# A hybrid decoder layer on one core: two tiles of the in-projection become a fifth Strassen pair, and quadrants of pairs are used from their banks

## The chip, the cores and the metric

The kernel runs on one core of a Trainium2 chip. The core has a matrix engine (TensorE, here PE, with its weight loads PEld), a vector engine (VectorE, DVE), a scalar engine (ScalarE, ACT), a general engine (GpSimd, POOL) and a queue that issues most DMAs (SyncE, SP). Each engine works off its own list of instructions in order; between engines there are semaphores. The metric is the device time of one execution in microseconds (us).

## What is computed

One layer over 1024 tokens of width 1024, in float32. The parts that matter here, shortened from the reference:

```python
u = rms_norm(x, norm1_g)
z = u @ w_in                       # 1024 -> 3584 columns, 28 tiles of 128
cb, cc, ch = split(z[:, :1536], 3) # convolution group, 512 each
rq, rk, rv, rg = split(z[:, 1536:], 4)
y_conv = cb * causal_dwconv3(cc * ch, conv_w)   # three taps along the tokens
y_conv = group_rms_norm(y_conv, conv_norm_g, 8)
o = chunkwise_retention(rotary(rq), rotary(rk) / sqrt(128), rv)   # 4 heads
y_ret = group_rms_norm(o, ret_norm_g, 4) * silu(rg)
x = x + concat(y_conv, y_ret) @ w_out
x = x + relu(rms_norm(x, norm2_g) @ w_up)**2 @ w_down
out = rms_norm(x, final_norm_g)
```

## The kernel before

Everything is held transposed: a tile is 128 columns of a product (on the partitions) by 1024 tokens, worked on in two halves of 512 tokens. A float32 product is made of three matmuls on high and low parts (hi x hi, hi x lo, lo x hi). A group of 12 matmuls is four k-tiles of 128 times these three, over 512 tokens; it is the unit of the order (the constant SLOT), and a weight piece of 128 x 512 (tile r, split into wh by ACT and wl by DVE or POOL) feeds one or more groups. A whole tile of the in-projection takes four groups: two halves by two of k. Two tiles can be made together with a 2 x 2 Strassen scheme (`pair_in`): seven products of one group each in place of eight groups, at the price of sums and differences of the weight pieces (POOL and DVE) and of the quadrants (DVE). A quadrant is one tile's half; n1 to n7 below are the seven products, taken in the order 1, 2, 5, 6, 3, 7, 4, alternately in banks of the pools pm and pr, of four banks each.

The input is not normalised before the projection; each token's norm factor is multiplied in behind it. R holds the factor of each token, R2 its square (in the buffer named ssq). So the gate takes z*R before its silu, b takes z*R, and the product c*h takes R2 once. The tiles 0 to 11 of the convolution come as c, h, b for each of four output tiles (f % 3 = 0, 1, 2); 12 to 19 are q and k; 20 to 23 are the gates of the four heads. IN_TURNS lists the turns behind q and k: 0, 1, 2, 3 and 20 as whole tiles, then four pairs, then tile 21; IN_END lists tiles 22 and 23, of which all first halves are made before the second halves. Beside the first turns PE works on the retention of heads 2 and 3; its small steps (transposes of line 663, tiny DVE operations on tile m for the heads' norm) stand between the groups.

What follows a tile runs in tasks: `conv_h` makes c*h*R2 and the three taps (cv), `conv_b` makes b*R*cv and asks for a group norm, `gate` makes the silu and multiplies it into the head's output o_n, `norm` makes a group's norm with two matmuls on PE (lines 483, 484) and a correction by DVE. `background` and `tick` set the order in which the tasks' steps are written behind each group, by a model clock of each engine; `yield (pool, dve)` leaves the engine to that model. The lists of the engines are then fixed.

The buffers for whole tiles are short, so o_n of heads 2 and 3 and the first two convolution outputs y0 and y1 are written to DRAM (`put_by`, tile sp) and fetched again (`get_back`, tile back). Before, all four returns stand behind pair (10, 11), ahead of tile 21. The out projection starts with the high and low parts yh and yl of all eight y, made by `split_y`; its first group takes y0 to y3, y0 first. Nearly every operation of ACT, DVE and POOL goes through the class Engine, whose line 74 the profile shows for it; nearly every matmul through `mm`, line 403; weight pieces are fetched at line 162.

Of the kernel before, what the change touches and what calls it, by code (L numbers as in the profile page):

```python
# [16 lines left out]
P = 128  # L17
# [22 lines left out]
IN_TURNS = [0, 1, 2, 3, 20, (4, 5), (6, 7), (8, 9), (10, 11), 21]  # L40
IN_END = [22, 23]
# [38 lines left out]
def hybrid_layer(  # L80
# [594 lines left out]
    a_of, cvs = {}, {}  # L675

    def conv_h(i, half, z, psum):

        a, sl = a_of[i], hs[half]
        eng = dve if psum else (yield (pool, dve))  # L680
        eng.tensor_mul(a[:, sl], a[:, sl], z)
        eng = yield (pool, dve)
        eng.tensor_mul(a[:, sl], a[:, sl], R2[:, sl])
        mark(("a", i, half), eng)
        if half:
            yield "a", i, 0
        yield (act,)
        if i not in cvs:
            cvs[i] = unit(s="cv")
        cv = cvs[i]  # L690
        w = [sm[:, CW + 3 * i + j : CW + 3 * i + j + 1] for j in range(3)]
        act.activation(cv[:, sl], a[:, sl], AF.Copy, scale=w[2])
        yield (dve,)
        for j in (1, 2):
            to = slice(max(sl.start, j), sl.stop)
            dve.scalar_tensor_tensor(
                cv[:, to], a[:, to.start - j : to.stop - j], w[2 - j], cv[:, to],
                ALU.mult, ALU.add,
            )
        mark(("cv", i, half), dve)  # L700

    def conv_b(i, half, z, out, psum):
        sl = hs[half]
        o = out[:, sl]
        eng = dve if psum else (yield (pool, dve))
        eng.tensor_mul(o, z, R[:, sl])
        yield "cv", i, half
        eng = yield (pool, dve)
        eng.tensor_mul(o, o, cvs[i][:, sl])
        y[i] = out  # L710

        def done(rt, less):
            yield (dve,)
            dve.scalar_tensor_tensor(o, o, less_g[:, i : i + 1], rt, ALU.mult, ALU.mult)
            yield (dve,)
            dve.scalar_tensor_tensor(o, less, 1.5, o, ALU.subtract, ALU.mult)
            mark(("y", i, half), dve)

        asked.append((o, blkr, 1.0 / 64, done, clock[eng], LATE * half))

    def gate(h, half, z, g, psum):
        sl = hs[half]
        eng = dve if psum else (yield (pool, dve))
        eng.tensor_mul(g[:, sl], z, R[:, sl])
        yield (act,)
        act.activation(g[:, sl], g[:, sl], AF.Silu)
        yield "o", h, half
        yield (dve,)
        o = o_n[h, half]
        dve.scalar_tensor_tensor(  # L730
            o[:, sl], g[:, sl], sm[:, RG + h : RG + h + 1], o[:, sl], ALU.mult, ALU.mult
        )
        y[4 + h] = o
        mark(("y", 4 + h, half), dve)

    def use(f, half, out, z, psum):

        if f >= 20:
            return gate(f - 20, half, z, out, psum)
        if f % 3 == 1:  # L740
            return conv_h(f // 3, half, z, psum)
        return conv_b(f // 3, half, z, out, psum)

    def whole(f):
        def evac(z):
            if f < 20 and f % 3 == 0:
                out = a_of[f // 3] = unit(s="a")
                for half, sl in enumerate(hs):
                    act.copy(out[:, sl], z[half])
                return  # L750
            out = None if f < 20 and f % 3 == 1 else unit(s="z")
            for half in range(2):
                spawn(use(f, half, out, z[half], True), clock[dve])

        tile_in(evac)
# [68 lines left out]
    def pair_in(fs):  # L824
        out = [unit(s="z") for _ in range(2)]
        (c11, c12), (acc, c22) = ([o[:, sl] for sl in hs] for o in out)
        for at, n in enumerate(UP_ORDER):
# [6 lines left out]
            ready = None  # L834
            if n == 1:
                act.copy(acc, b)
            if n == 2:
                dve.tensor_add(c11, acc, b)
                ready = 0, 0
            if n == 5:  # L840
                b5 = b
            if n in (6, 7, 4):
# [3 lines left out]
            if n == 7:  # L846
                dve.tensor_add(c22, acc, b5)
                ready = 1, 1
            if n == 3:
                dve.tensor_add(c12, c12, b)  # L850
                ready = 0, 1
            if n == 4:
                ready = 1, 0
            if ready:
                f, half, o = fs[ready[0]], ready[1], out[ready[0]]
                if f < 20 and f % 3 == 0:
                    a_of[f // 3] = o
                else:
                    spawn(use(f, half, o, o[:, hs[half]], False), clock[dve], LATE * half)
# [35 lines left out]
    for at, turn in enumerate(IN_TURNS):  # L895
        if isinstance(turn, tuple):
# [3 lines left out]
        if at == len(IN_TURNS) - 2:  # L900
            for h in (2, 3):
                force(("by", ("o", h)))
                o_n[h, 0] = o_n[h, 1] = get_back(("o", h))
            for i in range(2):
                force(("by", ("y", i)))
                y[i] = get_back(("y", i))
                got["back", i] = now[0] + 10.0
# [3 lines left out]
    for half in range(2):  # L911
        for f, (z, banks, pieces) in ends.items():
            for c in range(2):
# [10 lines left out]
                if c:  # L924
                    spawn(use(f, half, z, banks[half], True), clock[dve])
# [638 lines left out]
```

## Time and profile before

| | |
|---|---|
| three runs | 1071.92, 1071.01, 1069.68 us; median 1071.01 |
| profiled execution | 1070.03 us, span of its instructions 1068.1 us |
| granted clock of PE | 0.999 |
| busy in the span | PE 1054.8, PEld 879.2, DVE 870.8, ACT 463.6, POOL 561.6 us |
| pair (8, 9), pair (10, 11), tile 21, out projection begin at | 272.4, 291.4, 311.43, 344.97 us |

A row of a timeline gives start and length in us, engine, line, operation, what it writes <- what it reads, the shape, xN where N instructions of the kind follow each other, and in brackets how long the engine stood idle before and for whom. A row by groups gives count | busy us, mean ns of one | idle us before them. In rows on a tile the figures are ns, least/median/most. A row on DMAs gives the us from issue to landing, least/median/most.

### The profile page before, as it was taken

To read this page: it belongs to the slowest core of one execution; us is meant where nothing else is said; L and a number is where in the kernel's file an instruction comes from. 1 tells how busy PE (TensorE), PEld (TensorE's weight loads), DVE (VectorE), ACT (ScalarE), POOL (GpSimd) and SP (SyncE) were. 2 spreads that over 40 slices of the span, in tenths; PEclk is the share of its full clock that TensorE was granted. 3 is DMA by queue.
4 is the path that set the end of the run, shared out by engine and by line. 5 is a ranking of instruction groups with operands and counts; after the bars stand their busy time and mean duration, and the time that the engine had idled before them with its cause. 6 is when DMAs were issued, how large, how long until landed. Compare 5 with 4: busy or idle time off the path is not lost.

```text
span 1068.1 us, 13853 instructions
## 1 busy us (share of the span) xinstructions
PE 1054.8 (99%) x4860; PEld 879.2 (82%) x4860; DVE 870.8 (82%) x1231; ACT 463.6 (43%) x906; POOL 561.6 (53%) x381
## 2 busy tenths in 40 slices
PE   9999999999999999999999999999999999999997
PEld 8888888788888888788788888888888888888886
DVE  7446546799998665799999989999899899899955
ACT  8211445673437444443343433343443434334453
POOL 6334324367854233559458267277186295384552
PEclk9999999999999999999999999999999999999999
DMA  7121122122223733051221211211301201200204
GB/s 276 65 58 42 38 80 70 63 95 80 69 69 129 256 115 123 11 187 39 61 59 49 79 31 50 90 30 50 99 21 50 89 21 49 90 21 19 69 30 158
DMA packets 39685, 82.25 MB, mean 77 GB/s; under 512 B 4544, under 2 KB 5696, under 8 KB 39616
## 3 DMA queue, kind: packets, MB, share of 16 engines
q1 hardware_dynamic: 39328, 80.85, 23.5%
q8 instruction: 38, 0.62, 0.2%
q10 hardware_dynamic: 288, 0.52, 0.1%
q14 instruction: 31, 0.25, 0.1%
HBM read 71.92 MB, written 9.44 MB: 76 GB/s over the span
## 4 chain that ended last, share of the span: by engine, by line
PE 90%; DVE 6%; ACT 2%; issue 1%; POOL 1%; DVEq 0%; ACTq 0%; POOLq 0%
PE b L403 55%; PE b L1277 23%; PE b L357 4%; PE b L1386 4%; DVE t L74 1%; DVE wl L74 1%; DVE x L74 1%; DVE m L74 1%; ACT h L74 1%; DVE q L74 1%; DVE V L74 1%; PE b L339 0%; PE b L595 0%; PE b L1436 0%; PE b L246 0%
## 5 line engine op out<-in xcount | busy, mean ns | idle before, releaser
L74 ACT CAST wh<-r 128x512 fp32r<-128x512 f32 x286 | 176.6, 620 | 326.4 <-PE b L403 134.4
L403 PE MATMUL b<-U,wh 128*128 128x512 f32 x1024 | 315.8, 390 | 2.0 <-DVE x L74 1.2
L74 DVE TENSOR_TENSOR wl<-r,wh 128x512 fp32r<-128x512 f32 x250 | 232.8, 933 | 89.0 <-ACT wh L74 87.8
L74 POOL TENSOR_TENSOR r<-r,r 128x512 f32<-128x512 f32 x136 | 210.2, 1548 | 114.1 <-DVE wl L74 66.1
L1277 PE MATMUL b<-V,wh 128*128 128x512 f32 x784 | 242.0, 389 | 0.7 <-POOL V L74 0.4
L403 PEld LDWEIGHTS b<-U,wh 128*128 128x128 f32 x1024 | 191.7, 188 | 43.2 <-issue 2.4
L74 DVE TENSOR_TENSOR x<-x,b 128x512 f32<-128x512 f32 (+1 forms) x312 | 195.5, 673 | 28.8 <-PE b L1386 14.3
L403 PE MATMUL b<-U,wl 128*128 128x512 f32 x512 | 199.2, 389 | 0.0
L1277 PEld LDWEIGHTS b<-V,wh 128*128 128x128 f32 x784 | 147.1, 188 | 32.4 <-POOL V L74 0.9
L74 POOL TENSOR_TENSOR t<-t,t 128x512 f32<-128x512 f32 x70 | 106.3, 1523 | 96.4 <-ACT t L74 50.4
L1277 PE MATMUL b<-V,wl 128*128 128x512 f32 x392 | 152.5, 389 | 0.0
L74 POOL TENSOR_TENSOR wl<-r,wh 128x512 fp32r<-128x512 f32 x36 | 51.4, 1432 | 119.3 <-ACT wh L74 116.5
L403 PEld LDWEIGHTS b<-U,wl 128*128 128x128 f32 x512 | 96.1, 188 | 19.9
L403 PE MATMUL b<-uh,wh 128*128 128x512 f32 x304 | 102.3, 396 | 0.0
L403 PE MATMUL b<-ul,wh 128*128 128x512 f32 x304 | 100.5, 390 | 0.0
L403 PE MATMUL b<-uh,wl 128*128 128x512 f32 x304 | 100.2, 389 | 0.0
L1277 PEld LDWEIGHTS b<-V,wl 128*128 128x128 f32 x392 | 73.6, 188 | 15.2
L74 POOL TENSOR_TENSOR V<-t,V 128x512 fp32r<-128x512 f32 x35 | 49.6, 1418 | 67.0 <-ACT V L74 67.0
L74 DVE TENSOR_TENSOR t<-t,b 128x512 f32<-128x512 f32 x112 | 75.8, 677 | 1.7 <-POOL t L74 1.2
L74 ACT ACTIVATE t<-t 128x512 f32<-128x512 f32 x64 | 40.2, 631 | 81.2 <-DVE t L74 80.5
L74 DVE TENSOR_TENSOR V<-t,V 128x512 fp32r<-128x512 f32 x63 | 70.3, 1116 | 0.0
L403 PEld LDWEIGHTS b<-uh,wl 128*128 128x128 f32 x304 | 57.0, 188 | 12.3
(177 smaller groups left out, 1431.3 us busy)
## 6 DMA issues: line engine op xcount, KB each, us to landing
r<-w_up_t SPq DMA_DIRECT2D x64, 256.0 KB, 2.6
r<-w_down_t SPq DMA_DIRECT2D x56, 256.0 KB, 2.7
r<-w_in_t SPq DMA_DIRECT2D x48, 256.0 KB, 2.7
xt<-xT SPq DMA_DIRECT2D x16, 256.0 KB, 5.4
xs<-xT SPq DMA_DIRECT2D x8, 512.0 KB, 5.0
r<-w_out_t SPq DMA_DIRECT2D x16, 256.0 KB, 2.7
x<-xT SPq DMA_DIRECT2D x8, 512.0 KB, 7.9
k<-x SPq DMA_DIRECT2D x6, 512.0 KB, 3.0
```

The source lines that it names most:

```text
L74: return f(out, *args, **kw)
L357: nc.tensor.matmul(vb[i], a[k][:, i * P : (i + 1) * P], b[k // 2][:, vs], start=(k == 0 and a is uh and b is vh), stop=(k == KT - 1 and a ...
L403: nc.tensor.matmul(b, a[:, k, :], rhs(n, k)[r], start=(start and i == 0), stop=(stop and i == len(ops) - 1),)
L1277: nc.tensor.matmul(b, a, r, start=(i == 0), stop=(i == len(ops) - 1))
L1386: nc.tensor.matmul(z, a, b, start=(k == 0 and t == 0), stop=(k == 3 and t == 2))
```

## The change

1. IN_TURNS ends with the pair (21, 22); only tile 23 stays in IN_END.
2. In `pair_in`, a new `finish` leaves the quadrant that a product completes in that product's bank (or that of n5) for h, b and the gates: z*R, h*c and the taps read the bank. Only c goes to SBUF. The last two columns of the first half of c*h are copied to a small tile `edge`, from which the second half's taps read across the boundary, since the halves now lie in different banks. The same holds for whole tiles of h.
3. `conv_c` multiplies c by R2 as soon as c has been copied out, in place of the multiply of c*h.
4. In the norm's `done`, (less - 1.5)*rt is made in the bank, then o*g*bank; before, o*g*rt was made in SBUF, then multiplied by (bank - 1.5).
5. The returns of o2 and o3 stand ahead of the last turn, those of y0 and y1 behind it, with a planned 6 instead of 10 us until they can be used; U, the right sides of the pairs, is let go before these two.

```diff
--- before.py
+++ after.py
@@ -37,8 +37,8 @@
 IN_QK = [12, 13, 16, 17, 14, 15, 18, 19]
-IN_TURNS = [0, 1, 2, 3, 20, (4, 5), (6, 7), (8, 9), (10, 11), 21]
-IN_END = [22, 23]
+IN_TURNS = [0, 1, 2, 3, 20, (4, 5), (6, 7), (8, 9), (10, 11), (21, 22)]
+IN_END = [23]
 SLOT, LOOK, PE_MARGIN, LATE = 2.72, 3.2, 1.2, 0.0
 WARM = 10
 NORM_MARGIN, STEP_MARGIN, POOL_LATE = 6.5, 0.3, 1.0
@@ -672,16 +672,22 @@
                 mark(("retention", p), act)
-    a_of, cvs = {}, {}
-    def conv_h(i, half, z, psum):
+    a_of, cvs, edges = {}, {}, {}
+    def conv_c(i, half):
+        eng = yield (pool, dve)
         a, sl = a_of[i], hs[half]
-        eng = dve if psum else (yield (pool, dve))
-        eng.tensor_mul(a[:, sl], a[:, sl], z)
-        eng = yield (pool, dve)
         eng.tensor_mul(a[:, sl], a[:, sl], R2[:, sl])
-        mark(("a", i, half), eng)
+        mark(("c", i, half), eng)
+    def conv_h(i, half, z):
+        sl = hs[half]
+        yield "c", i, half
+        yield (dve,)
+        dve.tensor_mul(z, z, a_of[i][:, sl])
         if half:
             yield "a", i, 0
         yield (act,)
@@ -689,21 +695,29 @@
             cvs[i] = unit(s="cv")
         cv = cvs[i]
         w = [sm[:, CW + 3 * i + j : CW + 3 * i + j + 1] for j in range(3)]
-        act.activation(cv[:, sl], a[:, sl], AF.Copy, scale=w[2])
+        act.activation(cv[:, sl], z, AF.Copy, scale=w[2])
+        if not half:
+            edges[i] = xp.tile([P, 2], F32, tag="edge", name=nm("edge"), bufs=4)
+            act.copy(edges[i], z[:, H - 2 :])
+            mark(("a", i, 0), act)
         yield (dve,)
         for j in (1, 2):
-            to = slice(max(sl.start, j), sl.stop)
+            to = slice(sl.start + j, sl.stop)
             dve.scalar_tensor_tensor(
-                cv[:, to], a[:, to.start - j : to.stop - j], w[2 - j], cv[:, to],
-                ALU.mult, ALU.add,
+                cv[:, to], z[:, : H - j], w[2 - j], cv[:, to], ALU.mult, ALU.add
             )
+            if half:
+                to = slice(sl.start, sl.start + j)
+                dve.scalar_tensor_tensor(
+                    cv[:, to], edges[i][:, 2 - j :], w[2 - j], cv[:, to], ALU.mult, ALU.add
+                )
         mark(("cv", i, half), dve)
-    def conv_b(i, half, z, out, psum):
+    def conv_b(i, half, z, out):
         sl = hs[half]
         o = out[:, sl]
-        eng = dve if psum else (yield (pool, dve))
-        eng.tensor_mul(o, z, R[:, sl])
+        dve.tensor_mul(o, z, R[:, sl])
         yield "cv", i, half
         eng = yield (pool, dve)
         eng.tensor_mul(o, o, cvs[i][:, sl])
@@ -711,17 +725,16 @@
         def done(rt, less):
             yield (dve,)
-            dve.scalar_tensor_tensor(o, o, less_g[:, i : i + 1], rt, ALU.mult, ALU.mult)
+            dve.scalar_tensor_tensor(less, less, 1.5, rt, ALU.subtract, ALU.mult)
             yield (dve,)
-            dve.scalar_tensor_tensor(o, less, 1.5, o, ALU.subtract, ALU.mult)
+            dve.scalar_tensor_tensor(o, less, less_g[:, i : i + 1], o, ALU.mult, ALU.mult)
             mark(("y", i, half), dve)
         asked.append((o, blkr, 1.0 / 64, done, clock[eng], LATE * half))
-    def gate(h, half, z, g, psum):
+    def gate(h, half, z, g):
         sl = hs[half]
-        eng = dve if psum else (yield (pool, dve))
-        eng.tensor_mul(g[:, sl], z, R[:, sl])
+        dve.tensor_mul(g[:, sl], z, R[:, sl])
         yield (act,)
         act.activation(g[:, sl], g[:, sl], AF.Silu)
         yield "o", h, half
@@ -733,24 +746,30 @@
         y[4 + h] = o
         mark(("y", 4 + h, half), dve)
-    def use(f, half, out, z, psum):
-        if f >= 20:
-            return gate(f - 20, half, z, out, psum)
-        if f % 3 == 1:
-            return conv_h(f // 3, half, z, psum)
-        return conv_b(f // 3, half, z, out, psum)
+    def kind(f):
+        return "g" if f >= 20 else "chb"[f % 3]
+    def use(f, half, out, z):
+        if kind(f) == "g":
+            return gate(f - 20, half, z, out)
+        if kind(f) == "c":
+            return conv_c(f // 3, half)
+        if kind(f) == "h":
+            return conv_h(f // 3, half, z)
+        return conv_b(f // 3, half, z, out)
     def whole(f):
         def evac(z):
-            if f < 20 and f % 3 == 0:
-                out = a_of[f // 3] = unit(s="a")
+            out = None if kind(f) == "h" else unit(s="z")
+            if kind(f) == "c":
+                a_of[f // 3] = out
                 for half, sl in enumerate(hs):
                     act.copy(out[:, sl], z[half])
+                    spawn(use(f, half, out, None), clock[act], 4.0)
                 return
-            out = None if f < 20 and f % 3 == 1 else unit(s="z")
             for half in range(2):
-                spawn(use(f, half, out, z[half], True), clock[dve])
+                spawn(use(f, half, out, z[half]), clock[dve])
         tile_in(evac)
@@ -824,6 +843,15 @@
     def pair_in(fs):
         out = [unit(s="z") for _ in range(2)]
         (c11, c12), (acc, c22) = ([o[:, sl] for sl in hs] for o in out)
+        def finish(i, half, c, a, b, to):
+            f = fs[i]
+            if kind(f) == "c":
+                to = c
+                a_of[f // 3] = out[i]
+            dve.tensor_add(to, a, b)
+            spawn(use(f, half, out[i], to), clock[dve], LATE * half)
         for at, n in enumerate(UP_ORDER):
             if not got.get("pairs") and n in (5, 6, 7, 4):
                 for j in range(4):
@@ -831,32 +859,22 @@
             b = product(n, (pm, pr)[at % 2])
             slot()
             prepare()
-            ready = None
             if n == 1:
                 act.copy(acc, b)
             if n == 2:
-                dve.tensor_add(c11, acc, b)
-                ready = 0, 0
+                finish(0, 0, c11, acc, b, b)
             if n == 5:
                 b5 = b
-            if n in (6, 7, 4):
+            if n in (6, 7):
                 dve.tensor_add(acc, acc, b)
             if n == 6:
                 dve.tensor_add(c12, acc, b5)
             if n == 7:
-                dve.tensor_add(c22, acc, b5)
-                ready = 1, 1
+                finish(1, 1, c22, acc, b5, b5)
             if n == 3:
-                dve.tensor_add(c12, c12, b)
-                ready = 0, 1
+                finish(0, 1, c12, c12, b, b)
             if n == 4:
-                ready = 1, 0
-            if ready:
-                f, half, o = fs[ready[0]], ready[1], out[ready[0]]
-                if f < 20 and f % 3 == 0:
-                    a_of[f // 3] = o
-                else:
-                    spawn(use(f, half, o, o[:, hs[half]], False), clock[dve], LATE * half)
+                finish(1, 0, acc, acc, b, b)
             tick()
         got["pairs"] = now[0]
@@ -893,18 +911,19 @@
     for i in range(2):
         spawn(put_by(("y", i), lambda i=i: y[i], ("y", i, 0), ("y", i, 1)))
     for at, turn in enumerate(IN_TURNS):
+        if at == len(IN_TURNS) - 1:
+            for h in (2, 3):
+                force(("by", ("o", h)))
+                o_n[h, 0] = o_n[h, 1] = get_back(("o", h))
         if isinstance(turn, tuple):
             pair_in(turn)
         else:
             whole(turn)
-        if at == len(IN_TURNS) - 2:
-            for h in (2, 3):
-                force(("by", ("o", h)))
-                o_n[h, 0] = o_n[h, 1] = get_back(("o", h))
-            for i in range(2):
-                force(("by", ("y", i)))
-                y[i] = get_back(("y", i))
-                got["back", i] = now[0] + 10.0
+    U.clear()
+    for i in range(2):
+        force(("by", ("y", i)))
+        y[i] = get_back(("y", i))
+        got["back", i] = now[0] + 6.0
     for idx in range(KT):
         spawn(split_y(idx, 0))
     ends = {f: (unit(s="z"), [bank() for _ in hs], []) for f in IN_END}
@@ -922,7 +941,7 @@
                 if half:
                     prepare()
                 if c:
-                    spawn(use(f, half, z, banks[half], True), clock[dve])
+                    spawn(use(f, half, z, banks[half]), clock[dve])
                 tick()
     for half in range(2):
         while any(("split" if half == 0 else "y", idx, half) not in got for idx in range(KT)):
```

Three places in the built order follow. First SP's queue around the returns, before (back_2883 and back_2885 are o2 and o3, back_2887 and back_2889 are y0 and y1; r are weight pieces):

```order
L162 DMA r_2849<-w_out_t 128x512
L162 DMA r_2873<-w_out_t 128x512
L878 DMA back_2883<-sp_1993 128x1024
L878 DMA back_2885<-sp_1995 128x1024
L878 DMA back_2887<-sp_2223 128x1024
L878 DMA back_2889<-sp_2584 128x1024
L162 DMA r_2925<-w_out_t 128x512
L162 DMA r_2959<-w_out_t 128x512
```

and with the change (back_2898 and back_2900 are o2 and o3, back_3086 and back_3088 are y0 and y1):

```order
L162 DMA r_2891<-w_in_t 128x512
L896 DMA back_2898<-sp_1997 128x1024
L896 DMA back_2900<-sp_1999 128x1024
L162 DMA r_2921<-w_in_t 128x512
L162 DMA r_2948<-w_out_t 128x512
L162 DMA r_2975<-w_out_t 128x512
L162 DMA r_2990<-w_out_t 128x512
L162 DMA r_3011<-w_out_t 128x512
L162 DMA r_3043<-w_out_t 128x512
L162 DMA r_3075<-w_out_t 128x512
L896 DMA back_3086<-sp_2250 128x1024
L896 DMA back_3088<-sp_2567 128x1024
```

y0 and y1 moved behind seven weight pieces, of which r_3075 takes the buffer of r_2975. Second, ACT with the change, from behind the weight cast wh_3013 to wh_3077 (b_3019 and b_3052 are banks of norms, z_2902 and z_2903 the gates of tiles 21 and 22):

```order
L74 ACT_TABLE_LOAD
L74 ACTIVATE r_3022<-b_3019,eps 128x512
L74 ACTIVATE r_3023<-r_3022 128x512
L74 ACT_TABLE_LOAD
L74 ACTIVATE z_2902<-z_2902 128x512
L74 CAST wh_3045<-r_2948 128x512
L74 ACT_TABLE_LOAD
L74 ACTIVATE r_3055<-b_3052,eps 128x512
L74 ACTIVATE r_3056<-r_3055 128x512
L74 ACT_TABLE_LOAD
L74 ACTIVATE z_2903<-z_2903 128x512
L74 CAST wh_3077<-r_2975 128x512
```

The two norms and the silus of the pair's quadrants each load a table, and stand ahead of wh_3077; the casts of the two returns, yh_3138 and yh_3141, stand seven and eight rows further down. Third, DVE behind the first tile of h, whose halves are b_1573 and b_1574, with the change:

```order
L74 SCALAR_TENSOR_TENSOR m_1937<-m_1937,bq 128x2
L74 TENSOR_TENSOR m_1941<-m_1941 128x2
L74 SCALAR_TENSOR_TENSOR m_1941<-m_1941,m_1937 128x2
L74 SCALAR_TENSOR_TENSOR m_1941<-m_1941 128x2
L74 SCALAR_TENSOR_TENSOR cv_1855<-b_1574,sm,cv_1855 128x511
L74 SCALAR_TENSOR_TENSOR cv_1855<-edge_1857,sm,cv_1855 128x1
L74 SCALAR_TENSOR_TENSOR cv_1855<-b_1574,sm,cv_1855 128x510
L74 SCALAR_TENSOR_TENSOR cv_1855<-edge_1857,sm,cv_1855 128x2
```

and before:

```order
L74 SCALAR_TENSOR_TENSOR cv_1855<-a_1532,sm,cv_1855 128x511
L74 SCALAR_TENSOR_TENSOR cv_1855<-a_1532,sm,cv_1855 128x510
L74 SCALAR_TENSOR_TENSOR m_1935<-m_1935,bq 128x2
L74 TENSOR_TENSOR m_1939<-m_1939 128x2
L74 SCALAR_TENSOR_TENSOR m_1939<-m_1939,m_1935 128x2
L74 SCALAR_TENSOR_TENSOR m_1939<-m_1939 128x2
L74 SCALAR_TENSOR_TENSOR cv_1855<-a_1532,sm,cv_1855 128x512 x2
```

The taps of the second half read the bank b_1574 and the edge, where before they read SBUF tile a.

## Prediction

> **What bounds the kernel now.** I read the page first (busy time, shares of the chain), then the waits of TensorE (PE), then the windows by stage, last the timelines around the places that the change touches.
>
> ```profile
> span 1068.1 us, 13853 instructions
> PE 1054.8 (99%) x4860; PEld 879.2 (82%) x4860; DVE 870.8 (82%) x1231; ACT 463.6 (43%) x906; POOL 561.6 (53%) x381
> PE 90%; DVE 6%; ACT 2%; issue 1%; POOL 1%; DVEq 0%; ACTq 0%; POOLq 0%
> ...
> PE b L663 <- ACT h L74: 2.3, 5, 0.7
> ...
> 113.00:220.00 107.00, 104.97 (x595) 90.38 (x596) 66.64 (x157) 58.03 (x202) 39.02 (x28) 1.00 0.24 79
> 220.00:330.00 110.00, 110.00 (x487) 91.07 (x486) 99.99 (x112) 56.11 (x89) 75.47 (x50) 1.00 0.26 82
> 330.00:425.00 95.00, 95.00 (x421) 78.65 (x420) 62.26 (x81) 47.09 (x79) 34.02 (x24) 1.00 0.43 144
> 520.00:970.00 450.00, 449.99 (x1985) 372.28 (x1985) 421.11 (x586) 177.73 (x308) 258.84 (x173) 1.00 0.19 56
> ```
>
> The page gives PE 1054.8 of 1068.1 us. A row of waits gives what PE waited for, us in all, times, longest. A window row gives its length, then busy PE, weight load, VectorE (DVE), ACT and GpSimd (POOL), then the granted clock. From 220 to 425, where the pairs, tiles 21 to 23 and nearly all of the out projection run, PE is never idle (110.00 of 110, 95.00 of 95), and neither from 520 to 970. There a matmul less is its time less, while a DVE or POOL operation less is worth nothing to PE, although DVE itself is busy 99.99 of 110. Of the stretches that the change touches only the retention (113 to 220) has idle PE, 2.03 us, nearly all in front of line 663's transposes.
>
> **First term: twelve matmuls less.**
>
> ```profile
> 306.15 19.04 PE b L403 x84
> 325.64 2.72 PE b L403 x12
> 311.43 0.62 PE L403 MATMUL b<-uh,wh 128*128 128x512 f32 x2
> 344.97 0.39 PE L403 MATMUL b<-yh,wh 128*128 128x512 f32 x1
> ```
>
> The first two are steps of the chain of waits (start, length): 84 matmuls in 19.04 us, 12 in 2.72, so 0.2267 each. Tiles 21 and 22 took eight groups of 12 and a pair takes seven: 12 x 0.2267 = **2.72 us less**. The other two are from PE's timeline: tile 21 starts at 311.43, the out projection at 344.97. Call S the start of pair (21, 22). Its products come in the order 1, 2, 5, 6, 3, 7, 4, with two matmuls of a norm (0.45 us) behind 3 and behind 7, so product 3 ends at S+13.60, 7 at S+16.77, 4 at S+19.94, tile 23 at S+30.82 = 342.25: there the out projection is now due.
>
> **Second term: the wait that the change adds there.** Its first bank takes y0 and then y1, which now come back behind the pair. I follow the queues that must be through before: ACT from wh_3013 to wh_3077, POOL's wl_3078, then on SP r_3075 (whose buffer wl_3078 frees) and the two returns.
>
> ```profile
> 324.35 1.28 ACT L74 ACT_TABLE_LOAD   x1
> 328.11 0.69 ACT L74 ACTIVATE r<-b,eps 128x512 f32<-128x512 f32 x1
> 328.83 0.63 ACT L74 ACTIVATE r<-r 128x512 f32<-128x512 f32 x1
> 334.91 0.64 ACT L74 ACTIVATE z<-z 128x512 f32<-128x512 f32 x1
> 330.17 0.62 ACT L74 CAST yh<-back 128x512 fp32r<-128x512 f32 x1 [0.20 <-DMA back<-sp]
> ...
> L74 POOL TENSOR_TENSOR wl<-r,wh 128x512 fp32r<-128x512 f32 x4 | 5.6, 1439 | 6.9 <-ACT wh L74 6.9
> L74 POOL TENSOR_TENSOR yl<-back,yh 128x512 fp32r<-128x512 f32 x2 | 3.0, 1523 | 4.3 <-ACT yh L74 4.3
> ...
> 152.63 0.33 SPq L162 DMA_DIRECT2D r<-w_in_t  x1
> 153.01 0.90 SPq L793 DMA_DIRECT2D xs<-xT  x2
> 320.04 1.85 SPq L878 DMA_DIRECT2D back<-sp  x4
> ```
>
> wh_3013 takes the buffer that product 3's matmuls read, so it starts at S+13.65 and ends at 14.27. Behind it ACT has, up to the end of wh_3077, four table loads (4 x 1.28), two pairs of r (2 x 1.32), two silus (2 x 0.64) and two casts (2 x 0.62): 10.28, so S+24.55. wl_3078 by 1.29 to 1.44: 25.9. The issue of r_3075 (0.33), then y0's at 26.2 and y1's at 26.65 (the four returns took 1.85, so about 0.45 each). How long from issue to landing is bounded by two answers on pairs of the same 512 KB, each behind a weight tile's:
>
> ```profile
> DMA to landing us min/median/max: 3.5/4.3/5.2
> ...
> DMA to landing us min/median/max: 3.6/5.4/7.1
> ```
>
> The first is the xs pair at 153.01, with nothing close behind it; the second is the first two of the four returns at 320.04, with two more behind. The change issues two alone, so I take the xs pair's: y1 lands at 26.65 + 5.2 = S+31.85, ACT's yh_3141 ends at 32.5, POOL's yl_3142 at 33.8 (1.29) to 34.0 (1.52). PE wants y1's low part in the bank's fifth matmul, at S+30.82 + 4 x 0.2267 = 31.73. The wait is 2.1 to 2.3; by 7.1 us, 4.0 to 4.2; by a first landing's 3.6 us, 0.5. I take **2.3**, within 0.5 to 4.2. Before, the returns left 24 us ahead of the out projection and cost ACT 0.20. Queued behind ACT's yh_3141 are a silu and wh_3162, wanted by PE 5.44 us after the start of the out projection; cast and low part come about 3 us earlier than that, so nothing further is late. The x loads on SP follow too, for use at the end of the first bank.
>
> [...]
>
> **Third term: tile 3 behind the first tile of h.** The taps now read the bank, so tile 3's second group, in a bank of the h tile, must let DVE finish the taps.
>
> ```profile
> 209.51 0.16 DVE L74 SCALAR_TENSOR_TENSOR m<-m,m 128x2 f32<-128x2 f32 x1
> 209.70 0.16 DVE L74 SCALAR_TENSOR_TENSOR m<-m 128x2 f32<-128x2 f32 x1
> 209.78 1.53 DVE L74 SCALAR_TENSOR_TENSOR cv<-a,sm,cv 128x512 f32<-128x512 f32 x2
> 210.66 0.71 PE L403 MATMUL b<-uh,wh 128*128 128x512 f32 x2
> ```
>
> DVE's small m operations end at 209.86; the taps of the second half are then 0.6, an edge operation of about 0.1 and 0.6 (from a bank, with nothing of POOL's in the way; 1.53 for two before), to about 211.2, against PE's 210.66 and 0.3 more until its second bank is written: **+0.3**, bounds 0 and +0.6.
>
> **Fourth term: the squared norm moves from the product to c.**
>
> ```profile
> 193.57 1.27 POOL L74 TENSOR_TENSOR a<-a,ssq 128x512 f32<-128x512 f32 x1
> 194.90 1.19 DVE L74 SCALAR_TENSOR_TENSOR m<-m,m 128x2 f32<-128x2 f32 x1
> 197.00 0.44 PE L663 MATMUL b<-ident,h 128*128 128x128 f32 x2 [0.66 <-ACT h L74]
> ```
>
> While POOL multiplies, one of DVE's tiny m operations takes 1.19 instead of the 0.16 above, and PE then waits 0.66 for the h that follows. The multiply now comes some 20 us earlier, one half on POOL and one on DVE, and can delay m there in the same way. Bounds: -0.66 (the wait goes and none comes) and +0.7 (it stays and another of the kind comes). I take **0**: the same work for the same neighbours, elsewhere.
>
> **Edits costed at nothing.** Multiplies by R and ssq that leave POOL, operands that stay in a bank, the norm's factor in its bank: their time goes down or moves in 215 to 311, where PE covers them. The pair's additions, three weight casts and low parts less, four POOL sums more, edge copies: ACT has 56.11 of 110 busy and POOL 75.47. Without that cover one 512-column operation is 0.68 on DVE or 1.3 to 1.7 on POOL. The o2 and o3 returns are asked for ahead of the pair, and used behind it.
>
> **The sum:** -2.72 + 2.3 + 0.3 + 0 = **-0.1 us**. The profiled execution took 1070.03 (span 1068.1 and 1.93 around it), so 1069.9; the three runs have a median of 1071.01, 0.98 above it, so in their terms **1070.9**.
>
> **The rivals.** Within 0.2% (2.14 us) a measurement of this kernel can hardly tell from no change.
>
> *A, the forecast:* the saving is handed back at the out projection. With the wait from 1.3 (half way to the first landing's 0.5) to 4.2 and the rest as summed: -1.1 to +1.8, so 1069.9 to 1072.8. All three terms at their bounds at once would be -2.9 or +2.8. Chance 0.60.
>
> *B, the returns come in time:* y1 lands like a first transfer, 3.6 us, and the wait is 0.5; or r_3075 is let go earlier. Then -2.72 + 0.5 + 0.3 = -1.9, and with the retention's 0.66 gone -2.6: 1068.4 to 1069.1. For it speak the firsts (3.5, 3.6), against it every second. Chance 0.23.
>
> *C, on the other side: a bank held for the taps stalls PE within the pairs.* Pair (21, 22)'s third product, due at S+5.44 = 316.87, takes the bank of tile 10's second half, which now stays taken until DVE's taps have read it.
>
> ```profile
> 312.06 1.29 POOL L74 TENSOR_TENSOR z<-z,ssq 128x512 f32<-128x512 f32 x1 [3.46 <-DVE z L74]
> 313.39 0.73 ACT L74 ACTIVATE cv<-z,sm 128x512 f32<-128x512 f32 x1 [5.85 <-POOL z L74]
> 316.59 2.44 DVE L74 SCALAR_TENSOR_TENSOR cv<-z,sm,cv 128x512 f32<-128x512 f32 x2
> ```
>
> Before, these taps ended at 319.03. Were they as late now, PE would stand 2.1 us, and the pair with all behind it moves: -2.72 + 2.3 + 0.3 + 2.1 = +2.0, and up to +3.9 with the slow landing: 1073 to 1075. It decides once the taps end behind 316.87. Against it: POOL's multiply by ssq (312.06 to 313.35) is no longer in that chain, and the product whose quadrant it is ended two products and a norm (5.89) ahead of S, at 305.5, so DVE's addition and multiply, ACT's 0.73 and the taps can end by 309 to 312. Chance 0.14, other held banks included.
>
> *D, the order does not shorten PE* (an eighth product's work comes back as something else): 1072.5 to 1074. The built order has 7 groups of 12, so 0.03.
>
> **Chances.** Faster by over 0.2% needs B with the retention's wait gone, wholly or in part: 0.18 of its 0.23. Slower by over 0.2% takes C (0.11 of it), the upper half of D (0.02), or A with the 7.1 us landing and the other terms high (0.04): 0.17. Same: 0.65. The range reaches from B's lower end, 1068.3, into C, 1073.6.
>
> **What would show it.** Term one: from the pair's first matmul to tile 23's last 30.82 us, without a wait. Term two: in PE's timeline a wait of 1.5 to 4 us for yl or yh in the first bank of the out projection, ACT's yh<-back waiting for the DMA, the returns' landing at 3.6 and 5 to 7 us. Term three: a wait for DVE cv at tile 3's second bank. Term four: the sum of waits at line 663 near 2.3. C: a wait of PE for cv inside a pair. The forecast is wrong if the out projection starts without a wait, or if PE shows idle time between 220 and 340.

## The result, and the profile after

The changed kernel takes 1073.36 us (median of 20 runs, 1071.66 to 1074.44), the kernel before 1071.52 us (20 runs beside them, 1069.68 to 1074.06): a ratio of 1.0014, with a 95% interval from 1.0007 to 1.0020. It is slower by 1.8 us, which is less than the 0.2% of the forecast's "same" but clear of no change; the forecast was 0.1 us faster. The profiled execution took 1074.44, the longest of its 20, so a second profile stands beside it below.

The page of the changed kernel begins with

```profile
span 1071.6 us, 13872 instructions
```

and its waits of TensorE (us in all, times, longest) are, but for those that before has too:

```profile
PE b L663 <- ACT h L74: 2.3, 5, 0.7
...
PE b L403 <- DVE t L74: 1.1, 1, 1.1
...
PE b L403 <- ACT yh L74: 1.0, 1, 1.0
PE b L403 <- POOL yl L74: 0.9, 1, 0.9
PE b L357 <- DVE vh L74: 0.7, 1, 0.7
...
PE b L625 <- ACT h L74: 0.4, 1, 0.4
...
PE b L403 <- DVE yl L74: 0.2, 1, 0.2
PE b L403 <- DVE cv L74: 0.2, 1, 0.2
```

The waits for yh and yl at the out projection are the second term of the prediction, that for cv the third. New and not forecast are L625's wait for h, the wait for DVE t in the MLP (the layer's last part, with w_up and w_down), and DVE vh in the first 6 us. The same places in PE's timeline of the changed kernel:

```profile
5.91 1.16 PE L357 MATMUL b<-vh,uh 128*128 128x512 f32 x4 [0.72 <-DVE vh L74]
113.55 0.58 PE L663 MATMUL b<-ident,h 128*128 128x128 f32 x2 [0.30 <-ACT h L74]
181.14 0.49 PE L625 MATMUL b<-v,h 128*128 128x128 f32 x2 [0.43 <-ACT h L74]
183.33 0.44 PE L663 MATMUL b<-ident,h 128*128 128x128 f32 x2 [0.59 <-ACT h L74]
212.74 0.50 PE L403 MATMUL b<-uh,wh 128*128 128x512 f32 x1 [0.22 <-DVE cv L74]
345.45 0.50 PE L403 MATMUL b<-yh,wh 128*128 128x512 f32 x1 [1.02 <-ACT yh L74]
346.17 0.50 PE L403 MATMUL b<-yl,wh 128*128 128x512 f32 x1 [0.23 <-DVE yl L74]
348.06 0.50 PE L403 MATMUL b<-yl,wh 128*128 128x512 f32 x1 [0.86 <-POOL yl L74]
434.96 0.70 PE L403 MATMUL b<-U,wh 128*128 128x512 f32 x2 [0.47 <-DVE x L74]
438.62 0.70 PE L403 MATMUL b<-U,wh 128*128 128x512 f32 x2 [0.67 <-DVE x L74]
500.88 0.70 PE L403 MATMUL b<-U,wh 128*128 128x512 f32 x2 [1.11 <-DVE t L74]
518.67 0.70 PE L403 MATMUL b<-U,wh 128*128 128x512 f32 x2 [0.71 <-ACT t L74]
```

Since the order from the out projection on is the same in both, I cut the span at places that both have. "Retention" goes from line 663's first transpose behind 112 to the norm's matmul (line 483) behind tile 3, "out" from there to PE's first wait for DVE x (434.96 above), "MLP" from the second such wait (438.62) to 518.67. What is behind 518.67 took 552.9 us in both. The last column is the longest that one of six reloads (x<-k, 512 KB each, ahead of the MLP) took from issue to landing; it is the last of them. Below, each profile of the study, in us:

| kernel (label) | first transpose at | retention | out | MLP | reload's landing |
|---|---|---|---|---|---|
| before | 112.96 | 111.42 | 208.26 | 78.87 | 7.0 |
| before, second (again_before) | 113.06 | 111.41 | 208.25 | 79.38 | 7.7 |
| the change | 113.55 | 112.69 | 208.72 | 80.05 | 8.7 |
| the change, second (again_after) | 113.38 | 112.62 | 207.92 | 79.71 | 8.3 |
| early | 113.70 | 112.69 | 205.70 | 79.54 | 8.2 |
| early, second (again_early) | 113.42 | 112.69 | 205.70 | 79.38 | 7.5 |
| order23 | 113.40 | 112.58 | 206.79 | 79.41 | 7.6 |
| no_pair | 113.02 | 112.65 | 209.87 | 79.28 | 7.3 |
| norm_late | 114.30 | 112.60 | 210.83 | 79.63 | 8.4 |
| early_bank | 113.50 | 111.46 | 205.70 | 79.34 | 7.4 |
| early_bank, second (again_early_bank) | 113.09 | 111.50 | 205.70 | 80.18 | 8.8 |
| early_bank_sbuf | 112.90 | 111.60 | 205.70 | 79.41 | 7.7 |
| pair_early | 112.92 | 111.40 | 216.95 | 80.21 | 9.0 |
| quad_sbuf | 113.49 | 112.69 | 217.01 | 78.49 | 6.8 |

The change's profile is 3.5 us longer than before's (1071.6 - 1068.1): 0.59 ahead of the retention, 1.27 in it, 0.46 in out, 1.18 in the MLP. Only the second and third are put down to the change: the other two vary between two profiles of one kernel by as much as 0.41 (early_bank, ahead of the retention) and 0.84 (early_bank, the MLP).

### The profile page after: what moved, and what is told of

It reads as the page before. It is cut to its first block, busy times and chain, and to the rows that moved or that the text cites. A ratio compares the mean times of both kernels' runs of the same rounds, so it can differ in the third digit from the quotient of the medians.

```text
span 1071.6 us, 13872 instructions
## 1 busy us (share of the span) xinstructions
PE 1053.8 (98%) x4848; PEld 876.7 (82%) x4848; DVE 871.6 (81%) x1251; ACT 468.7 (44%) x916; POOL 558.8 (52%) x383
## 4 chain that ended last, share of the span: by engine, by line
PE 85%; DVE 7%; ACT 3%; POOL 2%; issue 2%; DMA 1%; DVEq 0%; SPq 0%; ACTq 0%; POOLq 0%
PE b L403 52%; PE b L1296 22%; PE b L357 4%; PE b L1405 4%; ACT h L74 1%; DVE wl L74 1%; DVE t L74 1%; DVE x L74 1%; DVE m L74 1%; POOL r L74 1%; POOL x L74 1%; DVE q L74 1%; DMA back<-sp 1%; DVE V L74 1%; PE b L339 0%
## 5 line engine op out<-in xcount | busy, mean ns | idle before, releaser
L403 PE MATMUL b<-U,wh 128*128 128x512 f32 x1056 | 325.6, 390 | 3.0 <-DVE x L74 1.1
L74 DVE TENSOR_TENSOR wl<-r,wh 128x512 fp32r<-128x512 f32 x243 | 224.1, 925 | 90.6 <-ACT wh L74 90.0
L74 POOL TENSOR_TENSOR r<-r,r 128x512 f32<-128x512 f32 x140 | 214.2, 1532 | 119.2 <-DVE wl L74 68.2
L403 PEld LDWEIGHTS b<-U,wh 128*128 128x128 f32 x1056 | 197.7, 188 | 45.4 <-issue 1.9
L403 PE MATMUL b<-U,wl 128*128 128x512 f32 x528 | 205.5, 389 | 0.0
L74 POOL TENSOR_TENSOR wl<-r,wh 128x512 fp32r<-128x512 f32 x46 | 63.3, 1378 | 138.6 <-ACT wh L74 136.5
L403 PE MATMUL b<-uh,wh 128*128 128x512 f32 x284 | 96.1, 397 | 0.2 <-DVE cv L74 0.2
L403 PE MATMUL b<-ul,wh 128*128 128x512 f32 x284 | 94.0, 390 | 0.0
L403 PE MATMUL b<-uh,wl 128*128 128x512 f32 x284 | 93.8, 390 | 0.0
L403 PEld LDWEIGHTS b<-uh,wl 128*128 128x128 f32 x284 | 53.3, 188 | 11.5
```

Source lines behind the costliest of these rows:

```text
L74: return f(out, *args, **kw)
L403: nc.tensor.matmul(b, a[:, k, :], rhs(n, k)[r], start=(start and i == 0), stop=(stop and i == len(ops) - 1),)
```

## The experiments

My theory W (three waits): the pair's 2.72 us is handed back by the wait for y0 and y1, and 1.2 us more is lost in the retention, by c's multiply, and at tile 3. Rival M: the MLP's wait is the change's own. The other rivals stand with the runs.

**The changed kernel again, and the kernel before again.** No edit.

> The changed kernel itself, a second profile. Theory W (three waits): the same three stand again: about 3.2 us at the start of the out projection (0.3 of it PE's restarts), about 0.8 net in the retention, about 0.4 at tile 3; together with 2.72 saved +1.7 us against the kernel before. The wait of 1.1 us before the MLP's group at 500.88 and the first 0.6 us at the start of the kernel were that execution's own and are gone or smaller. Rival M (the MLP): the 1.1 us stands again at the same place and belongs to the change.

> The kernel before itself, a second profile. Four profiles with the change in them all show PE waiting 0.4 to 1.1 us for DVE's t ahead of one group of the MLP (near 500), the first profile of before shows none there. Theory V (varies): that wait hangs on the landing of the six reloads x<-k ahead of it (last at 7.0 us in before's profile, 8.7 in the changed one's) and stands in this profile too, 0.4 to 1 us. Rival M: it belongs to the change, and is not here.

The changed kernel took 1.0019 of before (1.0010 to 1.0028). In its second profile retention (112.62) and out (207.92, with waits of 1.18 and 0.17 for yl) stand again; the MLP's wait is 0.88. Before's second profile has a wait at that place as well:

```profile
497.97 0.70 PE L403 MATMUL b<-U,wh 128*128 128x512 f32 x2 [0.53 <-ACT wh L74]
```

So rival M falls: before's first profile had been a short one. The six reloads (least, median, most from issue to landing) in the changed kernel's first profile:

```profile
DMA to landing us min/median/max: 3.4/6.3/8.7
```

and in before's second:

```profile
DMA to landing us min/median/max: 3.7/5.9/7.7
```

Over the fourteen profiles the MLP stretch follows the last landing: 78.49 at 6.8, 79.34 at 7.4, 79.54 at 8.2, 80.05 at 8.7, 80.21 at 9.0; and the same kernel has 8.2 and 7.5 (early), or 7.4 and 8.8 (early_bank).

**The returns earlier (early).** They are issued behind the pair's third product (n5), where the right side t1 is let go.

```diff
             if n == 5:
                 b5 = b
+                if fs == IN_TURNS[-1]:
+                    back_early()      # U.pop("t1"), then get_back of y0 and y1
...
     U.clear()
-    for i in range(2):
-        force(("by", ("y", i)))
-        y[i] = get_back(("y", i))
-        got["back", i] = now[0] + 6.0
```

> Only the returns of y0 and y1 moved ahead, to behind the pair's third product, where the right side t1 is let go. Theory W: they land some 15 us before the out projection, its wait of 3.2 us is gone, -1.4 to -1.5 us against the kernel before (+1.7 - 3.2). Rival Q (queue): the SP queue is held by the returns' buffers, weight pieces come late and PE waits for them in the pair or in tile 23; no gain against the changed kernel, +1 to +2 against before. Rival M: the out projection's wait was not what made it slower; also no gain.

Measured 0.9993 (0.9984 to 1.0001), 1071.07 against 1071.50. SP's queue in this kernel:

```profile
322.66 3.83 SPq L162 DMA_DIRECT2D r<-w_out_t  x2
326.58 0.86 SPq L905 DMA_DIRECT2D back<-sp  x2
```

The first matmuls of its out projection on PE's timeline, without a wait:

```profile
344.41 0.39 PE L403 MATMUL b<-yh,wh 128*128 128x512 f32 x1
344.64 0.39 PE L403 MATMUL b<-yl,wh 128*128 128x512 f32 x1
```

And the issue of the same two returns in the changed kernel, 13 us later:

```profile
339.65 0.86 SPq L896 DMA_DIRECT2D back<-sp  x2
```

The wait is gone. Out falls from 208.72 and 207.92 to 205.70, so it had cost 3.0 us in the one profile and 2.2 in the other. No weight piece came late (rival Q). Retention 1.28 and out -2.56 against before make -1.3, within the measured interval of -1.7 to +0.1.

**y2 and y3 first (order23).**

```diff
-                c == 0, c == 1,
+                c == 0, c == 1, (2, 3, 0, 1) if j == 0 and c == 0 and half == 0 else range(4),
```

> The changed kernel with one order swapped: the out projection's first group takes y2, y3 and then y0, y1, six matmuls (1.36 us) in front of the first one that needs a return. Theory W: that much of the wait is covered: 1.3 us less than the changed kernel, +0.4 to +0.6 against before; the waits for yh and yl still stand, shorter. Rival M or Q: the returns were not what held it; +1.8 as the changed kernel.

Measured 1.0002 (0.9993 to 1.0011): 0.2 us above before where the changed kernel was 1.8 above both times. Out is 206.79; of the wait's 2.2 to 3.0 us 1.1 are left. It reaches the same wait by another way than early, and agrees.

**c's squared norm behind c*h again (norm_late).**

```diff
 def conv_c(i, half):                       # now only marks c as ready
-        eng.tensor_mul(a[:, sl], a[:, sl], R2[:, sl])
 def conv_h(i, half, z):
         dve.tensor_mul(z, z, a_of[i][:, sl])
+        yield (dve,)
+        dve.tensor_mul(z, z, R2[:, sl])
```

> The multiply by R2 stands behind c*h again (now by DVE in the bank), for all tiles; all else as changed. Theory W: the retention's 0.43 and 0.59 us waits near 181 and 183 go, the 0.66 near 197 may come back: -0.8 us against the changed kernel, +0.9 against before. Rival B (bank): the two DVE multiplies (0.68 each) come between c*h and the taps, so tile 3's second bank is held 0.7 to 1.4 us longer: no gain, +1.7 against before.

Measured 1.0045 (1.0033 to 1.0057), 5.0 us slower than before: neither forecast reached that far. The waits at 181 and 183 are gone, as theory W has it, but tile 3 now waits as rival B has it:

```profile
213.42 0.47 PE L403 MATMUL b<-uh,wh 128*128 128x512 f32 x1 [2.54 <-DVE cv L74]
...
345.98 0.50 PE L403 MATMUL b<-yh,wh 128*128 128x512 f32 x1 [0.89 <-ACT yh L74]
348.17 0.50 PE L403 MATMUL b<-yl,wh 128*128 128x512 f32 x1 [1.69 <-DVE yl L74]
```

The retention stretch stays at 112.60, and out grows to 210.83, because DVE is later with yl. Another 1.4 us is PE at a granted clock of 0.50 behind these waits (last section). So this run cannot size the fourth term.

**The change without its pair (no_pair).**

```diff
-IN_TURNS = [0, 1, 2, 3, 20, (4, 5), (6, 7), (8, 9), (10, 11), (21, 22)]
-IN_END = [23]
+IN_TURNS = [0, 1, 2, 3, 20, (4, 5), (6, 7), (8, 9), (10, 11), 21]
+IN_END = [22, 23]                           # and all four returns behind pair (10, 11)
```

> The change without its pair: tiles 21 and 22 apart and all four returns where they were before; quadrants in banks, norm's factor in the bank and c's squared norm stay. Theory W: 0.8 (retention) + 0.4 (tile 3), so +1.2 us against before. Rival N: those edits cost nothing outside one execution: 0.

Measured 1.0019 (1.0011 to 1.0028), 2.2 us slower than before by the medians, 1071.50 and 1073.66. Retention has 1.23 us more than before, as forecast, so it isn't the pair's. Another 1.61 us stands in out, of which PE's timeline shows

```profile
314.39 0.47 PE L403 MATMUL b<-uh,wh 128*128 128x512 f32 x1 [1.17 <-DVE cv L74]
```

and DVE's timeline, among the taps that it waits for,

```profile
312.40 1.18 DVE L74 SCALAR_TENSOR_TENSOR cv<-edge,sm,cv 128x1 f32<-128x1 f32 x1
```

This is the prediction's rival C, a bank held for the taps, at tile 21: as a whole tile it takes its second bank at once, where pair (21, 22) takes that bank only with its third product. About 1 us of the wait is that one operation on the edge, which took 1.18 in place of 0.21 (at 313.70 in the changed kernel) while POOL was at a low part of a weight (312.29, 1.28 long). So the pair, beside saving twelve matmuls, takes away a wait that edit 2 brings without it.

**c read from the bank (early_bank).** On top of early:

```diff
-                    act.copy(out[:, sl], z[half])
-                    spawn(use(f, half, out, None), clock[act], 4.0)
+                    dve.tensor_mul(out[:, sl], z[half], R2[:, sl])
+                    mark(("c", f // 3, half), dve)
```

> The early returns, and in whole tiles c is multiplied by R2 by DVE as it is read from the bank (0.68 us each), in place of ACT's copy and a multiply of 1.3 to 1.8 us by POOL or DVE. Theory W: the multiply of 1.79 us that stood ahead of h near 178 is gone, and with it PE's 0.42 and 0.59 us of waits: 0.8 us less than with early returns alone, -1.3 to -1.5 us against before. Rival B: as with the multiply behind c*h, the time comes back at tile 3's bank: -0.5 us, no better than early.

Measured 0.9977 (0.9969 to 0.9986), 1068.83 against 1071.27: faster than both kernels by 2.4 us and more. DVE near the retention's steps, first in the changed kernel:

```profile
178.05 1.79 DVE L74 TENSOR_TENSOR z<-z,ssq 128x512 f32<-128x512 f32 x1
179.77 0.60 DVE L74 SCALAR_TENSOR_TENSOR h<-b,bk,causal 128x128 f32<-128x128 f32 x2
```

with the step of ACT that takes this h on to PE,

```profile
180.46 0.63 ACT L74 ACTIVATE h<-b,bz 128x128 f32<-128x128 f32 x2 [2.53 <-DVE h L74]
```

then DVE here:

```profile
172.66 1.27 DVE L74 TENSOR_TENSOR z<-b,ssq 128x512 f32<-128x512 f32 x2
...
178.51 0.60 DVE L74 SCALAR_TENSOR_TENSOR h<-b,bk,causal 128x128 f32<-128x128 f32 x2
```

In the changed kernel DVE's half of the multiply starts at 178.05, as POOL begins a subtraction of its own for U (178.01, 1.29 long); it takes 1.79 in place of 0.68 (DVE's multiply by ssq at 196.21 in before), and h stands behind it. ACT stood idle for this h (2.53), so the copies of c, which early_bank takes from ACT as well, are not what held it up. Read from the bank the two halves take 1.27 together, and PE has one wait of 0.24 behind them (at 177.15). Retention falls from 112.69 to 111.46, before's own length.

**c*h of whole tiles in SBUF again (early_bank_sbuf).** On top of early_bank:

```diff
-        dve.tensor_mul(z, z, a_of[i][:, sl])
+        if i < 2:
+            a = a_of[i][:, sl]
+            dve.tensor_mul(a, a, z)
+            z = a
+        else:
+            dve.tensor_mul(z, z, a_of[i][:, sl])
```

> As early_bank, and for the two whole tiles of h the product c*h goes to SBUF again, so that tile 3's bank waits for one multiply instead of the taps. Theory W: 0.4 us less than early_bank: -1.7 to -1.9 us against before; no wait of PE at tile 3. Rival B: the taps from SBUF beside POOL's work (1.5 us for two before) make DVE late elsewhere: as early_bank or worse.

Measured 0.9980 (0.9971 to 0.9988), no better than early_bank. Tile 3's wait is gone, but transposes of line 663 wait again right in front of it:

```profile
206.72 0.59 PE L663 MATMUL b<-ident,h 128*128 128x128 f32 x2 [0.82 <-ACT h L74]
210.44 0.58 PE L663 MATMUL b<-ident,h 128*128 128x128 f32 x2 [0.35 <-ACT h L74]
```

(In early_bank the first was 0.73, and there was no second.) Rival B's number is right, its mechanism isn't: the taps in front of tile 3 took as long as in early_bank (209.90 to 211.56, against 209.87 to 211.51). The built order gave POOL a subtraction for U there (207.84, 1.30 long) that DVE makes in early_bank, and the operation on m that stands ahead of the second wait's h took 0.83 beside it, against 0.15 in early_bank:

```profile
208.33 0.83 DVE L74 SCALAR_TENSOR_TENSOR m<-m,bq 128x2 f32<-128x2 f32 x1 [0.61 <-ACT h L74]
```

So this order gains nothing by taking the wait at tile 3 away; whether another one would, no run shows.

**The pair alone, with early returns (pair_early).** The kernel before with

```diff
-IN_TURNS = [0, 1, 2, 3, 20, (4, 5), (6, 7), (8, 9), (10, 11), 21]
-IN_END = [22, 23]
+IN_TURNS = [0, 1, 2, 3, 20, (4, 5), (6, 7), (8, 9), (10, 11), (21, 22)]
+IN_END = [23]                               # and the returns as in early
```

> The kernel before with the fifth pair alone, and the returns of y0 and y1 behind the pair's third product; R2 behind c*h, quadrants and norms as before. Theory W: the twelve matmuls, 2.72 us, with nothing given back in the retention or at tile 3: -2.5 us against before. Rival D (DVE): without the quadrants in the banks DVE and POOL are too late for the denser order, and PE waits in the pair, in tile 23 or at the out projection: 0 to -1 us.

Measured 1.0082 (1.0069 to 1.0096), 8.7 us slower: rival D, and far beyond what I gave it. At the out projection PE stands 6.6 us, though the returns had landed long before (issued at 327.34, at most 5.0 us to landing). ACT is late:

```profile
323.14 0.59 ACT L74 COPY z<-b 128x512 f32<-128x512 f32 x1 [4.37 <-DVE cv L74]
...
333.64 0.63 ACT L74 ACTIVATE z<-z 128x512 f32<-128x512 f32 x1 [3.12 <-DVE z L74]
...
337.87 0.63 ACT L74 ACTIVATE z<-z 128x512 f32<-128x512 f32 x1 [3.09 <-POOL z L74]
...
346.19 1.12 ACT L74 CAST yh<-back 128x512 fp32r<-128x512 f32 x2
```

ACT's copy of the pair's first product waits for a buffer that the taps of tile 10 still read, then its silus wait for z*R, from DVE and from POOL (1.74 us a multiply), and the casts of yh stand behind these in ACT's list.

**Only the quadrants in SBUF (quad_sbuf).** On top of early:

```diff
+            to = c
             if kind(f) == "c":
-                to = c
                 a_of[f // 3] = out[i]
```

> Early returns, and the quadrants of the pairs go to SBUF again in place of their banks; whole tiles, R2, the norm's factor and the engines of the multiplies by R as changed. The kernel before with pair and early returns alone was 8.7 us slower than before, with PE standing 6.6 us at the out projection behind ACT's and DVE's queues; early returns with all edits 0.4 faster. If it is the place of the quadrants that keeps those queues short (theory P): a good part of that wait is back, +3 to +6 us against before. If it is the rest, chiefly POOL's multiplies by R gone and the norm's factor in the bank (theory E): within 1 us of early, -0.5 to +0.5.

Measured 1.0069 (1.0055 to 1.0082), 7.5 us slower than before and 8 slower than early: theory P. ACT's same copy is the row to look at, here

```profile
325.73 0.58 ACT L74 COPY z<-b 128x512 f32<-128x512 f32 x1 [7.71 <-DVE cv L74]
```

and in early:

```profile
316.82 0.58 ACT L74 COPY z<-b 128x512 f32<-128x512 f32 x1
```

With its quadrants in SBUF, DVE's taps end 11 us later (325.70 against early's 314.73), and ACT, idle for 7.71 us ahead of the copy, has all later casts behind it: the next ran at 326.88, against 319.91 in early. Most of the 11 us is the place of the taps in DVE's list, not their length. ACT had cv ready for them at 316.45, but ten other operations of DVE's stand in front of the first tap,

```profile
324.03 0.74 DVE L74 SCALAR_TENSOR_TENSOR cv<-z,sm,cv 128x511 f32<-128x511 f32 x1
```

where in early none does. So theory P holds for this kernel together with its built order; what moved the taps in that order stays open. Out is 217.01, as in pair_early (216.95), which lacks edits 3 and 4 as well: those brought nothing here. In its profile out is 11.3 us longer than early's, more than the 8 of the times; PE's granted clock there was 0.50 from 354 to 358, and the execution's mean clock 0.995, where the other three have 0.999.

**Second profiles of early and early_bank.** No edit.

> Early returns, a second profile. The group of the MLP from 432 to 515 took 78.9 and 79.4 us in the two profiles of before, with the last reload x<-k landing after 7.0 and 7.7 us, and 79.3 to 80.1 in the others, with 7.3 to 8.7. Theory V: the landing is each execution's own: anything from 7 to 8.7 here, not again 8.2. Rival K: it is each kernel's own: 8.2 and 79.5 again.

> Early returns with c read from the bank, a second profile. Theory V: the last reload lands anywhere from 7 to 8.7 us after its issue. Rival K: 7.4 and 79.3 again, as in this kernel's first profile. The stretch from the retention to tile 4 takes 112.1 us again, as in before (112.0) and 1.2 less than in the changed kernel (113.3).

The last reload took 7.5 us in early (8.2 before) and 8.8 in early_bank (7.4 before): theory V. Retention and out came again to within 0.04 us.

## Why the prediction was wrong

The forecast was -0.1 us, the measurement is +1.8 (+0.75 to +2.1). By the stretches, which leave out what varies by execution, the change costs +1.7 in its first profile and +0.9 in its second. By the terms below the first is -2.56 + 3.02 + 0.48 + 0.79.

- **First term, -2.72: right.** From the pair's first matmul to the out projection's, early takes 30.86 us (313.55 to 344.41; the sum had 30.82), where before's tiles took 33.54 (311.43 to 344.97): 2.68 less. Out as a whole is 2.56 shorter (205.70 against 208.26), because early loses 0.11 ahead of the pair, from line 483's matmul to the pair's first (87.16 against 87.05); what lost it, I cannot say.
- **Second term, +2.3: the mechanism was right, the size within its bounds.** It cost 3.0 and 2.2. The queue came as worked out. The pair's first matmul, S, is

```profile
313.40 0.39 PE L403 MATMUL b<-uh,wh 128*128 128x512 f32 x1
```

and y0's return was issued at 339.65, which is S+26.25 (the forecast said 26.2). The landing set the difference. The two returns took, in the changed kernel's first profile,

```profile
DMA to landing us min/median/max: 5.1/5.5/5.9
```

and in its second

```profile
DMA to landing us min/median/max: 4.1/4.5/4.9
```

so y1's 5.9 and 4.9 lie on both sides of the 5.2 that I took. PE's idle time in the first is 2.11 (1.02 + 0.23 + 0.86); the other 0.9 is three restarts, about 0.3 each, which the sum left out (the first matmul behind a wait took 0.50 in place of 0.39, and the next began 0.34 behind it in place of 0.23).
- **Fourth term, 0: this is the step that failed. Third term, +0.3: right in its mechanism.** Together they measured +1.2 to +1.3. At the first matmul of tile 3, ahead of the wait for the taps, the changed kernel had lost 0.79 (212.04 - 113.55 against 210.66 - 112.96): the fourth term. The rest, 0.48, came at tile 3's second bank, within the third term's 0 to +0.6.

  "The same work for the same neighbours, elsewhere" was wrong. Now DVE's own half, stretched to 1.79, stands ahead of h in DVE's list, and PE waits twice for it, at 181 (0.43) and at 183 (0.59). The old wait of 0.66 went only by half: at 199 PE still waits 0.34, with POOL's multiply by ssq gone from there. That row was misread too: by the profile POOL had ended the multiply (at 194.84) when m began to take its 1.19 (at 194.90), and was at its next operation, on xs (194.81, 1.26 long). My upper bound of +0.7 for the move counted one such wait and was passed a little by the 0.79. early_bank shows the cause: take that multiply out of the gap and the 1.2 us are gone. Of the two terms the fourth is the one that decides: with c out of the way tile 3 still waits 0.22, and the stretch is as long as before.

  The sign that I had named for this term, a sum of waits at line 663 near 2.3, came true all the same (2.3 in both). The 0.59 at 183 had taken the place of a wait of 0.35 in front of tile 3 (at 210.32 before), the 0.43 fell on line 625, and a sum of idle time leaves out the restarts.
- **"Edits costed at nothing": wrong in both orders.** I priced the quadrants in banks as work that PE covers. In the old order they bring a wait of 1.17 at tile 21 (no_pair). In the new one quad_sbuf has them in SBUF and loses 8 us to early: there PE had no cover for taps that come 11 us later. What I should have asked was what the pair would cost without them.
- **The prediction's rivals.** B (landing in time, the retention's wait gone) did not come. C did not come in the changed kernel, whose taps end at 314.70, 4.1 us ahead of S+5.44 = 318.84; it came at tile 21 in no_pair, 1.17 us. D fell: from the pair to the out projection the order is 2.68 us shorter.

## What to carry to other kernels

When a stage is full on TensorE, saved matmuls are saved time only as far as the next stage's first operands are ready; follow the queue in front of them, as here to a weight piece that held two returns back, and issue them behind the earliest step that frees their buffers (here worth 2.2 to 3.0 us). Operations moved into a gap of another stage have to be judged by what stands behind them in the same engine's list there, and at their stretched duration (here 1.79 us in place of 0.68). And edits that look covered may be what makes a denser order possible: cost them in the new order too.

## What the runs showed of the hardware

**A gap in PE's work can cost twice.** In pair_early PE stood 4.26 us, and its granted clock was then 0.50 for some 10 us, with two more waits (0.56 and 1.81) in them, until some 3.6 us behind the last (353.36 to 356.93) (length, then busy PE, weight load, DVE, ACT, POOL, then the clock):

```profile
338.00:342.00 4.00, 4.00 (x20) 3.30 (x19) 2.84 (x5) 3.92 (x6) 0.00 (x0) 1.00 0.30 81
346.80:348.00 1.20, 0.80 (x1) 0.29 (x1) 1.20 (x2) 1.20 (x3) 1.13 (x1) 0.50 0.00 0
354.00:356.00 2.00, 2.00 (x6) 1.59 (x5) 2.00 (x3) 0.00 (x0) 0.43 (x1) 0.50 0.03 2
358.00:360.00 2.00, 2.00 (x11) 1.63 (x10) 2.00 (x5) 2.00 (x5) 0.00 (x0) 1.00 0.99 331
```

A matmul then took 0.63 in place of 0.39, one behind the other every 0.43 in place of 0.23. It also came without a long gap: in norm_late waits of 0.89 and 1.69, with one matmul between them, and of 0.18 three matmuls later, were followed by a clock of 0.50 from 349.3 to 352.5, 1.4 us more on top of the waits (seven matmuls, 0.43 apart in place of 0.23). In the changed kernel's first profile, whose gaps of 1.02, 0.23 and 0.86 have one and three matmuls between, it stayed at 1.00. (Three of that kernel's 20 runs have a mean granted clock of 0.996, as norm_late's profile has, where the others have 0.998 or 0.999; whether it fell there too, no trace shows.) Ahead of its fall pair_early has 4.26 us without a matmul; in norm_late the longest stretch nearly idle was 3.1 us (345.09 to 348.17), with a single matmul in it. How long a gap has to be for the clock to fall, these runs do not show.

**A row of transfers lands differently each time.** Six reloads of 512 KB, issued in the same order, had the last land between 6.8 and 9.0 us after its issue, and PE's time in the following stage moved with it from 78.5 to 80.2 us. A single profile of either kernel is no measure of a change of 1 or 2 us; cutting it at common places, and profiling twice, was.
